# Recurrent heads that take one step per half tile of projections, with their matmuls pinned in program order on TensorE

## The chip, the cores and the metric

The kernel runs on one core of a Trainium2 chip. The metric is the time of one execution on the device in microseconds (us). The engines of a core run side by side, each with its own queue of instructions that it takes strictly in order: TensorE (PE) multiplies matrices into eight PSUM banks, VectorE (DVE) and GpSimd (POOL) do elementwise work, ScalarE (ACT) does copies, casts and functions, and SyncE (SP) issues the DMAs. An instruction that needs the result of another engine waits for it at the head of its queue, and all that is queued behind it waits too.

## The reference, cut to what matters

The model has two layers. Each layer is a feed-forward block, a mixer and a second feed-forward block, over 512 prompt tokens and 8 sample tokens (one step each for 8 sequences), which share the weights; together they are 520 columns. The mixer projects x once, runs attention, a Mamba-2 scan and an HGRN2 recurrence beside each other, projects each to the model's width, gates and adds them. The change touches the HGRN2 branch and the projections around it:

```python
h = x @ p['w_in'] + p['b_in']
q, k, v, mz, mxbc, mdt, hq, hf, hi, hg, gates = _split_cols(h)
...
oh, nhg = _hgrn2(hq, hf, hi, lb, hg_prev)       # per head: S = exp(g) * S + k^T i,  o = q S
yh = (_rmsnorm(oh, p['hg_norm_w']).reshape(b, T, HG_WIDTH) * jax.nn.silu(hg.astype(jnp.float32))).astype(x.dtype)
...
merged = g_att * (ya @ p['w_br_att']) + g_ssm * (ym @ p['w_br_ssm']) + g_hg * (yh @ p['w_br_hg'])
```

HGRN2 has 4 heads (head 0 to 3 below) of 128 x 128 state. For the prompt it starts from zero and is computed in chunks of 128 tokens; for the 8 samples it is one step from a given state each.

## The kernel before

**Tiling.** Activations lie transposed, 128 channels by 520 columns, and every product is made in two halves of 260 columns; the sample columns 512 to 519 are in half 1. `gemm` (L165) makes a half tile from three matmuls per block of 128 (L176 to L178: the high part of x by the high part of the weight, the low part of x by the high, the high by the low). `lin` (L477) takes the next weight tile, makes the half tiles and has `evac` carry each to SBUF; `lin_bias` and `lin_silu` are the two evacuations. A half tile of projections is 24 matmuls of 128 x 260.

**The heads.** `hgrn_lin` (L571) first projects ten units (the forget gates of the four heads, q, i and the gate of head 0 and 1) by halves, hands the tiles out and then is a generator over the other six units. `attention_lin` (L1049) follows with six units (k, v, four q). `hgrn_head` (L601) is a generator for one head: gate functions, products on POOL and DVE that build `hk` and `hep`; five levels of four matmuls each (`level`, L638, matmuls at L646), after each a masked copy and two multiplies on DVE (L666 is the second one of level 0, L674 that of the others); transposes of i and `hk` with their copies on ACT (L685, L686), the state products on PE (L692), the states `hst` on DVE (L693, L696), the outputs (L703 and, from `hst`, L706), squares on ACT (L711), normalising on DVE (L712 to L714), transposes (L722), and the gate (L724), after which `split` (L502) casts to a high part `yhh` on ACT (L505) and a low part on DVE (L506).

**The sample steps.** `hgrn_sample` (L728) copies the head's sample columns on DVE (L733), transposes f, k, q on PE (L737), copies them as `r8` on ACT (L739), sends them to DRAM and reads them back spread over all partitions into `smp` tiles (of which there are 6), in two halves of four sequences. Each half is one POOL multiply (L748), four DVE operations that add k by i (L751), one POOL multiply by q (L754) and four ACT sums (L757) into `s_o`. When all four steps are done `hgrn_sample_out` (L759) squares (L762), makes the mean on PE (L764), normalises on DVE (L765 to L769), and `split_samples` casts to the sample columns of the four `yhh` tiles (L513), which the first merge's half 1 reads.

**What sets the order.** `weave` (L555) runs in rounds: a round takes one step of the projections (`fill`) and then, at a higher priority, `pace` steps of every head or sample step that is alive; a head h joins at round `HG_ROUNDS[h]`, a sample step at `HG_SAMPLES[h]`. A step ends at a `yield`. Then comes `merge` (L1225) with the attention pairs woven in: for each of eight output tiles and each half a gate (24 matmuls) and the branch product over the four `yhh` / `yhl` pairs (12 matmuls). The program's order is not yet the queues' order: a tile scheduler places every instruction by its priority and its own idea of when its inputs are ready, and lets later ones pass. Only an instruction that is pinned with `keep_in_program_order` stays behind the one that the program issued before it on its engine. The PSUM banks are four of tag `g` (projections, merge), three of tag `s` (heads, attention) and one of tag `x` (sample steps).

```python
HG_ROUNDS = (0, 2, 4, 5)
HG_SAMPLES = (5, 6, 8, 10)
...
        self.weave(lins, starts, 22 - len(self.MIX_HEAD), 2)
        with self.early(3):
            self.hgrn_sample_out(l)
```

Of the kernel before, what the change touches and what calls it, by code (L numbers as in the profile page):

```python
# [43 lines left out]
HK = DT // 2  # L44
HG_ROUNDS = (0, 2, 4, 5)
AT_ROUNDS = (0, 0, 3, 3)
HG_SAMPLES = (5, 6, 8, 10)

# [77 lines left out]
class Kernel:  # L126
# [349 lines left out]

    def lin(self, evac, m=P, halves=(0, 1)):  # L477
        wt = self.w.get()
        for half in halves:
            c0, c1 = HALVES[half]  # L480
            p = self.bank()
            self.gemm(p, wt, self.xs, half, m=m)
            with self.early(1):
                evac(p[:m, : c1 - c0], c0, c1)

    def lin_bias(self, out, bias, scale=1.0, halves=(0, 1)):
        self.lin(lambda p, c0, c1: self.nc.scalar.activation(out[:, c0:c1], p, AF.Identity, bias=bias, scale=scale), halves=halves)

    def lin_silu(self, out, hbias, halves=(0, 1)):

        nc = self.nc

        def evac(p, c0, c1):
            u = self.half_tile()[:, : c1 - c0]
            t = self.half_tile()[:, : c1 - c0]
            nc.scalar.activation(u, p, AF.Identity, bias=hbias, scale=0.5)
            nc.scalar.activation(t, p, AF.Tanh, bias=hbias, scale=0.5)
            nc.vector.scalar_tensor_tensor(out[:, c0:c1], t, 1.0, u, op0=ALU.add, op1=ALU.mult)

        self.lin(evac, halves=halves)  # L500

# [25 lines left out]
    def mixer(self, l):  # L527
        self.hg_out, self.ms_out, self.at_out, self.mgs = [], [], [], []
        self.sp = {n: self.sm(32, "s_" + n) for n in ("f", "k", "q", "i", "sg", "z", "aq", "ak", "av", "y", "o")}
        self.sp["x"] = self.sm(48, "s_x")  # L530
        self.scv, self.pcv = self.sm(144, "scv"), self.sm(18, "pcv")
        self.nc.sync.dma_start(self.scv.rearrange("p (j b w) -> p j b w", b=8, w=3), self.ap["sconv"][l])
        lins = self.hgrn_lin(l)
        st = next(lins)
        aq = {}
        lins = itertools.chain(lins, self.attention_lin(l, aq))
        head = lambda h: self.hgrn_head(l, h, st)
        smp = lambda h: self.hgrn_sample(l, h, st)
        pair = lambda i: self.attention_pair(l, i, aq)

        starts = [(r, head(h)) for h, r in enumerate(HG_ROUNDS)] + [(r, smp(h)) for h, r in enumerate(HG_SAMPLES)]
        self.weave(lins, starts, 22 - len(self.MIX_HEAD), 2)
        with self.early(3):
            self.hgrn_sample_out(l)
        self.mg = self.wide("mg")
        self.weave(self.merge(l, 0, self.hg_out), [(r, pair(i)) for i, r in enumerate(AT_ROUNDS)], DT, 2)
        with self.early(3):
            self.attention_sample(l)
        self.mamba(l)
        self.weave(self.merge(l, 1, self.at_out), [], DT, 0)  # L550
# [18 lines left out]


    def hgrn_lin(self, l):  # L571
        nc = self.nc
# [4 lines left out]
        def unit(u, halves=(0, 1)):  # L577
            hb = dp[:, u : u + 1]
            if u < 4:
                self.lin_bias(T[u], pr[:, 48 + u : 49 + u], halves=halves)  # L580
                return
            h, kind = (u - 4) // 3, (u - 4) % 3
# [3 lines left out]
            if kind == 1:  # L586
                self.lin_bias(d[h], pr[:, 48 + u : 49 + u], halves=halves)
            else:
                self.lin_silu(d[h], hb, halves)

        for half in (0, 1):
            for u in self.MIX_HEAD:
                unit(u, (half,))
        yield T, q, it, sg
        for u in range(16):
            if u in self.MIX_HEAD:
                continue
            unit(u)
            yield

    def hgrn_head(self, l, h, st):  # L601
# [36 lines left out]
        def level(i):  # L638
# [5 lines left out]
            for c in range(4):  # L644
                out = p[:m, c * n : c * n + n]
                nc.tensor.matmul(  # L646
                    out.rearrange("p (b w) -> p b w", w=w) if i else out,
# [17 lines left out]
        nc.vector.tensor_tensor(ep3, ep3, tf.unsqueeze(2).to_broadcast([P, 64, 8]), op=ALU.mult)  # L665
        nc.vector.tensor_tensor(em3, em3, ts.unsqueeze(2).to_broadcast([P, 64, 8]), op=ALU.mult)  # L666
        w = 8
        for i in range(1, 5):
# [21 lines left out]
        for c in range(4):  # L690
            cs = slice(c * P, (c + 1) * P)
            nc.tensor.matmul(pst[:, cs], lhsT=ktok[:, cs], rhs=itok[:, cs], start=True, stop=True)  # L692
        nc.vector.tensor_copy(st[:, :P], pst[:, :P])  # L693
# [7 lines left out]
        for c in range(4):  # L701
            cs = slice(c * P, (c + 1) * P)
            nc.tensor.matmul(po[:, cs], lhsT=att[:, c, :], rhs=itok[:, cs], start=c == 0, stop=False)  # L703
# [16 lines left out]
        for c in range(4):  # L720
            cs = slice(c * P, (c + 1) * P)
            nc.tensor.transpose(pt[:, cs], o[:, cs], self.ident)  # L722
        yv = self.sum_slot("hy")[:, :TP]
# [4 lines left out]
    def hgrn_sample(self, l, h, st):  # L728
# [121 lines left out]
    def mamba(self, l):  # L850
# [16 lines left out]
        for j in range(4):  # L867
            self.lin_silu(z[j], dp[:, 28 + j : 29 + j])
            nc.vector.tensor_copy(self.sp["z"][:, 8 * j : 8 * j + 8], z[j][:, TP:])
# [179 lines left out]
    def attention_lin(self, l, aq):  # L1049
        nc = self.nc  # L1050
        pr = self.par[l]
        k = self.slot(name="ak")
        self.lin_bias(k, pr[:, 48 + 16 : 48 + 17])
        nc.vector.tensor_copy(self.sp["ak"][:, :8], k[:, TP:])
        nc.sync.dma_start(self.ap["o_pk"][l], k[:, TP - P : TP])
        yield
        v = self.slot(name="av")
        self.lin_bias(v, pr[:, 48 + 17 : 48 + 18])
# [3 lines left out]
        yield  # L1062
        for i in range(4):
            q = self.slot(name="aq")
            self.lin_bias(q, self.qb[l][:, i : i + 1], scale=0.125)
            nc.vector.tensor_copy(self.sp["aq"][:, 8 * i : 8 * i + 8], q[:, TP:])
            aq[i] = q
            yield

# [442 lines left out]
```

## Time and profile before

| | |
|---|---|
| median of 3 runs | 2611.08 us (2609.08 to 2611.87) |
| the profiled execution | 2615.0 us |
| its span on the core | 2613.2 us |
| PE busy | 2544.7 us (97%) |
| DVE busy | 1949.0 us (75%) |
| ACT busy | 1251.0 us (48%) |
| POOL busy | 681.6 us (26%) |

The profile is of one execution. The timeline of an engine lists start (us from the span's start), duration, engine, line, operation, tiles as out<-in, shapes and count; in square brackets stands the idle time ahead of it and what ended that. A table of waits groups the idle time of an engine by the line that waited and the line waited for. Windows give the busy time of every engine in a stretch and the granted clock of TensorE as a share of its full speed. Tile names carry no numbers in the trace. The recurrent heads of layer 0 lie at 424.5 to 560 us, those of layer 1 at 1723.6 to 1859 us.

### The profile page before, as it was taken

The numbers are of one execution on the slowest core, as the hardware profiler recorded it, in microseconds if no ns is written. First come the engines' busy times: TensorE is split into PE (matmuls) and PEld (weight loads), VectorE is DVE, ScalarE is ACT, GpSimd is POOL, SyncE is SP. The second block draws the span as 40 slices with busy tenths as digits, with TensorE's granted clock in tenths as the row PEclk, the third lists the DMA queues.
The fourth block names the chain that finished last, engine by engine and source line by source line (L and its number), as shares of the span: only waits on it lengthen the run. The fifth ranks groups of instructions, "written<-read, shape, count | busy, mean of one in ns | idle before, by whom it ended". The sixth has DMA issues, their size and how long they took to land.

```text
span 2613.2 us, 51867 instructions
## 1 busy us (share of the span) xinstructions
PE 2544.7 (97%) x20784; PEld 2477.7 (95%) x20784; DVE 1949.0 (75%) x3690; ACT 1251.0 (48%) x2358; POOL 681.6 (26%) x635
## 2 busy tenths in 40 slices
PE   8999999999999999999989999999999999999997
PEld 8999999898989999999989999999989899999997
DVE  8795888854685588868897858978546845978596
ACT  6343566443534473434663534754435344635255
POOL 2121243300143441212331212433001434312124
PEclk9999999999999999999999999999999999999999
DMA  5331446412242343232532414564123423333233
GB/s 209 111 129 66 142 162 217 149 66 82 99 138 91 122 138 107 88 114 82 186 132 86 146 57 142 175 213 138 60 86 111 138 90 123 135 100 106 89 121 123
DMA packets 134066, 318.17 MB, mean 122 GB/s; under 512 B 20452, under 2 KB 56516, under 8 KB 133824
## 3 DMA queue, kind: packets, MB, share of 16 engines
q1 hardware_dynamic: 133824, 314.86, 35.9%
q8 instruction: 163, 2.67, 0.4%
q14 instruction: 79, 0.65, 0.1%
HBM read 302.93 MB, written 11.88 MB: 120 GB/s over the span
## 4 chain that ended last, share of the span: by engine, by line
PE 72%; DVE 16%; DMA 4%; issue 3%; ACT 2%; POOL 2%; SPq 0%; POOLq 0%; ACTq 0%; DVEq 0%
PE g L176 15%; PE g L177 15%; PE g L178 15%; PE g L382 5%; PE g L384 5%; PE g L383 5%; DVE wl L91 3%; PE s L382 2%; PE s L384 2%; PE s L383 2%; DVE y L225 1%; DMA ws<-in_w_gu 1%; PE s L1098 1%; DMA smp<-r8d 1%; DVE ht L200 1%
## 5 line engine op out<-in xcount | busy, mean ns | idle before, releaser
L176 PE MATMUL g<-xh,wh 128*128 128x260 f32 (+1 forms) x2336 | 671.8, 288 | 6.6 <-ACT xh L1375 5.9
L178 PE MATMUL g<-xh,wl 128*128 128x260 f32 (+1 forms) x2336 | 669.8, 287 | 2.9 <-DVE wl L91 2.8
L177 PE MATMUL g<-xl,wh 128*128 128x260 f32 (+1 forms) x2336 | 669.5, 287 | 0.3 <-DVE xl L1376 0.3
L90 ACT CAST wh<-ws 128x1024 fp32r<-128x1024 f32 (+1 forms) x382 | 389.7, 1025 | 382.2 <-PE g L177 256.4
L91 DVE TENSOR_TENSOR wl<-ws,wh 128x1024 fp32r<-128x1024 f32 (+1 forms) x382 | 466.5, 1223 | 124.6 <-ACT wh L90 123.6
L176 PEld LDWEIGHTS g<-xh,wh 128*128 128x128 f32 (+1 forms) x2336 | 441.5, 189 | 16.4 <-issue 6.1
L178 PEld LDWEIGHTS g<-xh,wl 128*128 128x128 f32 (+1 forms) x2336 | 441.4, 189 | 10.1 <-issue 4.1
L177 PEld LDWEIGHTS g<-xl,wh 128*128 128x128 f32 (+1 forms) x2336 | 441.4, 189 | 7.9 <-issue 4.6
L73 ACT CAST wh<-ws 128x1024 fp32r<-128x1024 f32 (+1 forms) x288 | 265.4, 941 | 290.9 <-PE g L177 161.7
L178 PE MATMUL g<-hh,wl 128*128 128x260 f32 x1408 | 396.0, 283 | 0.0
L177 PE MATMUL g<-hl,wh 128*128 128x260 f32 x1408 | 395.9, 283 | 0.0
L176 PE MATMUL g<-hh,wh 128*128 128x260 f32 x1408 | 391.9, 282 | 1.9 <-DVE y L251 1.9
L74 DVE TENSOR_TENSOR wl<-ws,wh 128x1024 fp32r<-128x1024 f32 (+1 forms) x288 | 317.9, 1110 | 90.0 <-ACT wh L73 88.5
L105 POOL TENSOR_TENSOR ws<-ws 128x512 f32<-128x512 f32 x72 | 128.3, 1783 | 643.1 <-DMA ws<-in_w_gu 251.7
L176 PEld LDWEIGHTS g<-hh,wh 128*128 128x128 f32 x1408 | 262.9, 188 | 2.4 <-DVE y L251 2.3
L177 PEld LDWEIGHTS g<-hl,wh 128*128 128x128 f32 x1408 | 264.8, 188 | 0.1
L178 PEld LDWEIGHTS g<-hh,wl 128*128 128x128 f32 x1408 | 264.5, 188 | 0.2
L382 PE MATMUL g<-xh,wh 128*128 128x260 f32 x864 | 245.6, 285 | 3.3 <-ACT wh L73 3.0
L383 PE MATMUL g<-xl,wh 128*128 128x260 f32 x864 | 244.3, 284 | 0.0
L384 PE MATMUL g<-xh,wl 128*128 128x260 f32 x864 | 241.8, 283 | 0.0
L382 PEld LDWEIGHTS g<-xh,wh 128*128 128x128 f32 x864 | 163.4, 189 | 5.8 <-ACT wh L73 4.8
L382 PE MATMUL g<-sx,wh 128*128 128x260 f32 x576 | 163.3, 284 | 4.1 <-ACT wh L73 4.1
(407 smaller groups left out, 5712.2 us busy)
## 6 DMA issues: line engine op xcount, KB each, us to landing
ws<-in_w_gu SPq DMA_DIRECT2D x208, 512.0 KB
ws<-in_w_in SPq DMA_DIRECT2D x132, 512.0 KB
ws<-in_w_dn SPq DMA_DIRECT2D x96, 512.0 KB
ws<-in_w_out SPq DMA_DIRECT2D x32, 512.0 KB
ws<-in_w_dn SPq DMA_DIRECT2D x32, 384.0 KB
smp<-r8d SPq DMA_DIRECT2D x48, 256.0 KB
ws<-in_w_br SPq DMA_DIRECT2D x24, 512.0 KB
smp<-in_hgr SPq DMA_DIRECT2D x16, 256.0 KB
```

Of the source, the lines that this page charges most:

```text
L73: nc.scalar.copy(h[:, :n], s[:, :n])
L74: nc.vector.tensor_tensor(lo[:, :n], s[:, :n], h[:, :n].bitcast(F32), op=ALU.subtract)
L90: nc.scalar.copy(h[:, :n], s[:, :n])
L91: nc.vector.tensor_tensor(lo[:, :n], s[:, :n], h[:, :n].bitcast(F32), op=ALU.subtract)
L105: nc.gpsimd.tensor_tensor(pa[:, b], u[:, a], u[:, b], op=ALU.add)
L176: nc.tensor.matmul(out, lhsT=h[:, wc], rhs=xh[:, c0:c1], start=st, stop=False)
L177: nc.tensor.matmul(out, lhsT=h[:, wc], rhs=xl[:, c0:c1], start=False, stop=False)
L178: nc.tensor.matmul(out, lhsT=lo[:, wc], rhs=xh[:, c0:c1], start=False, stop=en)
L200: nc.vector.tensor_tensor(s1, self.y[0][:, c0:c1] if n == 1 else s1, y, op=ALU.add)
L382: nc.tensor.matmul(out, lhsT=h[:, wc], rhs=xh, start=first and k == 0, stop=False, **go)
L383: nc.tensor.matmul(out, lhsT=h[:, wc], rhs=xl, start=False, stop=False, **go)
L384: nc.tensor.matmul(out, lhsT=lo[:, wc], rhs=xh, start=False, stop=k == HK - 1, **go)
```

## The change

The projections become a generator that yields after each half tile (`lin_steps`), so a round is a half tile and not a tile: 24 rounds and not 12, and a head or sample step takes one step a round and not two. The rounds at which they join are rewritten. Two more `yield`s are put in: in a head after level 0's two multiplies, in a sample step after its three copies. All matmuls and transposes of the heads and the sample steps go through `mm` and `tr`, which pin them in program order. No instruction is added or removed.

```diff
-HG_ROUNDS = (0, 2, 4, 5)
+
+HG_ROUNDS = (0, 3, 7, 10)
 AT_ROUNDS = (0, 0, 3, 3)
-HG_SAMPLES = (5, 6, 8, 10)
+HG_SAMPLES = (8, 11, 14, 18)
...
-    def lin(self, evac, m=P, halves=(0, 1)):
+    def lin(self, *args, **kw):
+        for _ in self.lin_steps(*args, **kw):
+            pass
+
+    def lin_steps(self, evac, m=P, halves=(0, 1)):
         wt = self.w.get()
         for half in halves:
...
                 evac(p[:m, : c1 - c0], c0, c1)
+            yield
...
-        self.weave(lins, starts, 22 - len(self.MIX_HEAD), 2)
+        self.weave(lins, starts, 2 * (22 - len(self.MIX_HEAD)), 1)
+        for _ in lins:
+            pass
...
+    def mm(self, *args, **kw):
+        self.tc.keep_in_program_order(self.nc.tensor.matmul(*args, **kw))
+
+    def tr(self, *args):
+        self.tc.keep_in_program_order(self.nc.tensor.transpose(*args))
...
-                nc.tensor.matmul(
+                self.mm(
                     out.rearrange("p (b w) -> p b w", w=w) if i else out,
...
         nc.vector.tensor_tensor(em3, em3, ts.unsqueeze(2).to_broadcast([P, 64, 8]), op=ALU.mult)
+        yield
         w = 8
...
-                nc.tensor.transpose(p[:, cs], src[:, cs], self.ident)
+                self.tr(p[:, cs], src[:, cs], self.ident)
...
-            nc.tensor.matmul(po[:, cs], lhsT=qp[:, cs], rhs=st[:, ps], start=False, stop=c == 3)
+            self.mm(po[:, cs], lhsT=qp[:, cs], rhs=st[:, ps], start=False, stop=c == 3)
...
             nc.vector.tensor_copy(sp[n][:, sl], t[h][:, TP:])
+        yield
 
         p = self.bank("x")
         for k, n in enumerate(("f", "k", "q")):
-            nc.tensor.transpose(p[:8, k * P : (k + 1) * P], sp[n][:, sl], self.ident)
+            self.tr(p[:8, k * P : (k + 1) * P], sp[n][:, sl], self.ident)
```

What this does to the queues shows in their order. The first matmuls of level 0 of head 0 moved from row 3373 of PE's queue to row 3509; outside the heads' section and the first merge the order is the same. Line numbers of the kernel after are moved by the edit (L176 is L177, L751 is L766), and every pinned matmul carries the line of `mm` (L582), every pinned transpose that of `tr` (L585).

PE, layer 0, the transposes of the last sample step (`x`, from the small tiles `s_f`, `s_k`, `s_q`) before, among projections (`g_6419`) and level 1 of head 2 (`hep_6003`, `hk_5959`):

```order
L176 MATMUL g_6419<-xh_78,wh_6018 128x260
L646 MATMUL s_6104<-hep_6003,hk_5959 128x64 x4
L692 MATMUL s_6163<-hit_6082,hkt_6083 128x128 x4
L177 MATMUL g_6419<-xl_79,wh_6018 128x260
L178 MATMUL g_6419<-xh_78,wl_6019 128x260
L176 MATMUL g_6419<-xh_78,wh_6018 128x260
L177 MATMUL g_6419<-xl_79,wh_6018 128x260
L737 MATMUL x_6860<-ident_1015,s_f_4733 8x128
L737 MATMUL x_6860<-ident_1015,s_k_4734 8x128
L737 MATMUL x_6860<-ident_1015,s_q_4735 8x128
L178 MATMUL g_6419<-xh_78,wl_6019 128x260
```

The same transposes now (`x_6788`), with the last head's state products (`s_6720`), outputs (`s_6759`) and the first merge's product (`g_7041`):

```order
L177 MATMUL g_7041<-yhh_6662,wh_6909 128x260
L582 MATMUL s_6720<-hit_6666,hkt_6667 128x128 x4
L582 MATMUL s_6759<-hit_6666,att1_1044 128x128 x4
L178 MATMUL g_7041<-yhl_6663,wh_6909 128x260
L179 MATMUL g_7041<-yhh_6662,wl_6910 128x260
L582 MATMUL s_6759<-hst_6719,hep_6207 128x128 x3
L585 MATMUL x_6788<-ident_1015,s_f_4733 8x128
L585 MATMUL x_6788<-ident_1015,s_k_4734 8x128
L585 MATMUL x_6788<-ident_1015,s_q_4735 8x128
L585 MATMUL s_6844<-ident_1015,ho_6767 128x128 x4
L1091 MATMUL s_7097<-ident_1015,av_6402 128x128 x4
```

They moved from row 3809 of PE's queue to row 4126, behind the last head's output products.

PE, layer 0, the first branch product of half 1 (`g_7082`, which reads the sample columns of `yhh`) before, behind a whole gate (`g_7055`):

```order
L177 MATMUL g_7055<-xl_79,wh_6800 128x260
L178 MATMUL g_7055<-xh_78,wl_6801 128x260
L176 MATMUL g_7082<-yhh_5989,wh_6904 128x260
L177 MATMUL g_7082<-yhl_5990,wh_6904 128x260
L178 MATMUL g_7082<-yhh_5989,wl_6905 128x260
```

And now, with the attention's scores (L1111) and the mean of the sample output (`x_6968`) ahead of it:

```order
L1111 MATMUL s_7142<-ak_6222,aq_6538 128x256
L1111 MATMUL s_7147<-ak_6222,aq_6686 128x128
L779 MATMUL x_6968<-ssq_6966,inv_hg_1031 128x32
...
L1111 MATMUL s_7166<-ak_6222,aq_6686 128x256
L1146 MATMUL s_7301<-ident_1015,asc_7105 128x128
L177 MATMUL g_7082<-yhh_6081,wh_6909 128x260
L177 MATMUL g_7177<-xh_78,wh_7004 128x260
L178 MATMUL g_7177<-xl_79,wh_7004 128x260
```

Between the last sample transposes and this product there stood 320 rows before, and 24 now; the next gate (`g_7177`) stands behind it.

DVE, layer 0, the last head's states (`hst`) before, with the last sample multiply (L751) 68 rows ahead:

```order
L514 TENSOR_TENSOR yhl_6659<-s_o_4743,yhh_6658 128x8
L506 TENSOR_TENSOR yhl_6659<-hy_6656,yhh_6658 128x512
L693 COPY hst_6662<-s_6663 128x128
L1178 COPY qm_1040<-s_aq_4739 64x8 x2
L696 SCALAR_TENSOR_TENSOR hst_6662<-hst_6662,tw128_6521,s_6663 128x128 x3
```

And now, the multiplies of sample step 2 (`smp`) directly ahead:

```order
L766 SCALAR_TENSOR_TENSOR smp_6522<-smp_6524,s_i_4736,smp_6522 128x128 x4
L738 SCALAR_TENSOR_TENSOR hy_6660<-s_6655,par0_1046,hsg_5632 128x512
L92 TENSOR_TENSOR wl_7356<-ws_7353,wh_7355 128x1024
L514 TENSOR_TENSOR yhl_6663<-hy_6660,yhh_6662 128x512
L766 SCALAR_TENSOR_TENSOR smp_6615<-smp_6617,s_i_4736,smp_6615 128x128 x4
L707 COPY hst_6719<-s_6720 128x128
L710 SCALAR_TENSOR_TENSOR hst_6719<-hst_6719,tw128_6608,s_6720 128x128 x3
```

The states moved behind the sample multiplies that were long done before.

## Rows read from the trace of the kernel before

**Rows 1.** Page part 1: busy time, share of the span, instructions of each engine.

```profile
PE 2544.7 (97%) x20784; PEld 2477.7 (95%) x20784; DVE 1949.0 (75%) x3690; ACT 1251.0 (48%) x2358; POOL 681.6 (26%) x635
```

**Rows 2.** Windows of the heads' section in layer 0 and 1: length, then busy times.

```profile
core 0: us, PE busy (x) PEld busy (x) DVE busy (x) ACT busy (x) POOL busy (x), PEclk, DMA share, GB/s
424.50:560.00 135.50, 127.04 (x1056) 124.08 (x1054) 105.73 (x277) 63.13 (x195) 42.76 (x49) 0.99 0.48 151
...
1723.60:1859.20 135.60, 127.75 (x1063) 124.39 (x1062) 107.11 (x280) 63.91 (x196) 42.34 (x49) 0.99 0.48 154
```

**Rows 3.** Waits of PE: us in total, times, longest.

```profile
PE s L646 <- DVE hk L666: 7.7, 5, 2.5
...
PE s L646 <- DVE hk L674: 4.3, 6, 1.2
...
PE x L737 <- DVE s_q L733: 2.5, 2, 1.2
```

**Rows 4.** Timelines of five engines, layer 0: the last sample step and its reader.

```profile
496.93 0.27 PE L737 MATMUL x<-ident,s_f 128*8 128x128 f32 x1
...
499.65 0.45 ACT L739 COPY r<-x 8x384 f32<-8x384 f32 x1
...
506.82 1.33 POOL L748 TENSOR_TENSOR smp<-smp 128x512 f32<-128x512 f32 x1 [1.43 <-DMA smp<-r8d]
...
517.30 0.34 DVE L751 SCALAR_TENSOR_TENSOR smp<-smp,s_i 128x128 f32<-128x128 f32 x1
...
517.77 1.27 POOL L754 TENSOR_TENSOR smp<-smp 128x512 f32<-128x512 f32 x1 [4.16 <-DVE newton L242]
...
528.47 0.25 DVE L769 SCALAR_TENSOR_TENSOR s_o<-s_o,par,s_sg 128x32 f32<-128x32 f32 x1
...
529.22 0.38 ACT L513 CAST yhh<-s_o 128x8 fp32r<-128x8 f32 x3
...
554.08 0.28 PE L176 MATMUL g<-yhh,wh 128*128 128x260 f32 x1
```

**Rows 5.** Timeline of PE: level products, two projection matmuls, the longest wait.

```profile
424.50 1.06 PE L646 MATMUL s<-hep,hk 128*128 128x128 f32 x8
...
425.31 0.36 PE L178 MATMUL g<-xh,wl 128*128 128x260 f32 x1
...
514.74 0.28 PE L176 MATMUL g<-xh,wh 128*128 128x260 f32 x1
514.86 0.28 PE L177 MATMUL g<-xl,wh 128*128 128x260 f32 x1
...
517.52 1.61 PE L646 MATMUL s<-hep,hk 128*128 128x64 f32 x8 [2.38 <-DVE hk L666]
```

**Rows 6.** Timelines of ACT and DVE: sample step 2, the last head's states.

```profile
479.50 0.47 ACT L739 COPY r<-x 8x384 f32<-8x384 f32 x1
...
494.83 1.13 DVE L751 SCALAR_TENSOR_TENSOR smp<-smp,s_i 128x128 f32<-128x128 f32 x4
...
547.64 0.28 DVE L693 COPY hst<-s 128x128 f32<-128x128 f32 x1
...
548.21 1.12 DVE L696 SCALAR_TENSOR_TENSOR hst<-hst,tw,s 128x128 f32<-128x128 f32 x3
```

**Rows 7.** Timelines of DVE and POOL: one multiply with POOL busy and idle.

```profile
492.16 1.73 POOL L748 TENSOR_TENSOR smp<-smp 128x512 f32<-128x512 f32 x1
...
492.67 1.77 DVE L666 TENSOR_TENSOR hk<-hk,ts 128x512 f32<-128x512 f32 x1
...
516.70 0.67 DVE L666 TENSOR_TENSOR hk<-hk,ts 128x512 f32<-128x512 f32 x1
```

**Rows 8.** Timeline of DVE: an operation of the attention's scores.

```profile
568.28 0.48 DVE L1104 CUSTOM_DVE_ANT_0 asc<-s,abias,par 128x256 f32<-128x256 f32 x1
```

**Rows 9.** Window behind the longest wait; the granted clock is the third last number.

```profile
517.89:521.30 3.41, 3.41 (x18) 3.41 (x18) 3.27 (x8) 1.51 (x9) 1.15 (x1) 0.50 0.22 81
```

More of the change, by code (lines that the diff above doesn't have):

```diff
@@ L484, in lin @@
                 evac(p[:m, : c1 - c0], c0, c1)
+            yield
     def lin_bias(self, out, bias, scale=1.0, halves=(0, 1)):
-        self.lin(lambda p, c0, c1: self.nc.scalar.activation(out[:, c0:c1], p, AF.Identity, bias=bias, scale=scale), halves=halves)
+        return self.lin_steps(
+            lambda p, c0, c1: self.nc.scalar.activation(out[:, c0:c1], p, AF.Identity, bias=bias, scale=scale), halves=halves
+        )
     def lin_silu(self, out, hbias, halves=(0, 1)):
@@ L498, in evac @@
             nc.vector.scalar_tensor_tensor(out[:, c0:c1], t, 1.0, u, op0=ALU.add, op1=ALU.mult)
-        self.lin(evac, halves=halves)
+        return self.lin_steps(evac, halves=halves)
     def split(self, y, name, slot=None):
@@ L579, in unit @@
             if u < 4:
-                self.lin_bias(T[u], pr[:, 48 + u : 49 + u], halves=halves)
-                return
+                return self.lin_bias(T[u], pr[:, 48 + u : 49 + u], halves=halves)
             h, kind = (u - 4) // 3, (u - 4) % 3
@@ L586, in unit @@
             if kind == 1:
-                self.lin_bias(d[h], pr[:, 48 + u : 49 + u], halves=halves)
-            else:
-                self.lin_silu(d[h], hb, halves)
+                return self.lin_bias(d[h], pr[:, 48 + u : 49 + u], halves=halves)
+            return self.lin_silu(d[h], hb, halves)
         for half in (0, 1):
             for u in self.MIX_HEAD:
-                unit(u, (half,))
+                yield from list(unit(u, (half,)))[1:]
         yield T, q, it, sg
         for u in range(16):
[L596 to L599, printed above, removed]
+            if u not in self.MIX_HEAD:
+                yield from unit(u)
     def hgrn_head(self, l, h, st):
@@ L691, in hgrn_head @@
             cs = slice(c * P, (c + 1) * P)
-            nc.tensor.matmul(pst[:, cs], lhsT=ktok[:, cs], rhs=itok[:, cs], start=True, stop=True)
+            self.mm(pst[:, cs], lhsT=ktok[:, cs], rhs=itok[:, cs], start=True, stop=True)
         nc.vector.tensor_copy(st[:, :P], pst[:, :P])
@@ L702, in hgrn_head @@
             cs = slice(c * P, (c + 1) * P)
-            nc.tensor.matmul(po[:, cs], lhsT=att[:, c, :], rhs=itok[:, cs], start=c == 0, stop=False)
+            self.mm(po[:, cs], lhsT=att[:, c, :], rhs=itok[:, cs], start=c == 0, stop=False)
         for c in range(1, 4):
             cs, ps = slice(c * P, (c + 1) * P), slice((c - 1) * P, c * P)
-            nc.tensor.matmul(po[:, cs], lhsT=qp[:, cs], rhs=st[:, ps], start=False, stop=c == 3)
+            self.mm(po[:, cs], lhsT=qp[:, cs], rhs=st[:, ps], start=False, stop=c == 3)
         o = self.sum_slot("ho")[:, :TP]
@@ L721, in hgrn_head @@
             cs = slice(c * P, (c + 1) * P)
-            nc.tensor.transpose(pt[:, cs], o[:, cs], self.ident)
+            self.tr(pt[:, cs], o[:, cs], self.ident)
         yv = self.sum_slot("hy")[:, :TP]
@@ L867, in mamba @@
         for j in range(4):
-            self.lin_silu(z[j], dp[:, 28 + j : 29 + j])
+            for _ in self.lin_silu(z[j], dp[:, 28 + j : 29 + j]):
+                pass
             nc.vector.tensor_copy(self.sp["z"][:, 8 * j : 8 * j + 8], z[j][:, TP:])
@@ L1052, in attention_lin @@
         k = self.slot(name="ak")
-        self.lin_bias(k, pr[:, 48 + 16 : 48 + 17])
+        yield from self.lin_bias(k, pr[:, 48 + 16 : 48 + 17])
         nc.vector.tensor_copy(self.sp["ak"][:, :8], k[:, TP:])
         nc.sync.dma_start(self.ap["o_pk"][l], k[:, TP - P : TP])
-        yield
         v = self.slot(name="av")
-        self.lin_bias(v, pr[:, 48 + 17 : 48 + 18])
+        yield from self.lin_bias(v, pr[:, 48 + 17 : 48 + 18])
         nc.vector.tensor_copy(self.sp["av"][:, :8], v[:, TP:])
@@ L1061, in attention_lin @@
         aq["k"], aq["v"] = k, v
-        yield
         for i in range(4):
             q = self.slot(name="aq")
-            self.lin_bias(q, self.qb[l][:, i : i + 1], scale=0.125)
+            yield from self.lin_bias(q, self.qb[l][:, i : i + 1], scale=0.125)
             nc.vector.tensor_copy(self.sp["aq"][:, 8 * i : 8 * i + 8], q[:, TP:])
             aq[i] = q
-            yield
     def attention_pair(self, l, i, aq):
```

## The prediction

> **What bounds the kernel now.** I read the share of busy time first: TensorE (PE) is busy 97% of the span and VectorE (DVE) 75% [rows 1]. Shares over the whole span say little about one stage, so the next view is busy time by stretch. The recurrent heads run from 424.5 to 560 us in layer 0 and again from 1723.6 us in layer 1. There PE is busy 127.04 of 135.50 us and 127.75 of 135.60, so it idles 8.5 and 7.9 us, 16.3 together [rows 2]. The table of PE's waits says for what: L646, the products of the levels, on DVE's `hk` (7.7 and 4.3 us) and L737, the transposes of the sample steps, on `s_q` (2.5), 14.5 of the 16.3 us [rows 3]. So the change can win at most 16.3 us, 0.6%, by better placing, unless it speeds up PE itself, and it removes no instruction.
>
> The second thing to read is how long the work beside PE takes, since a pinned instruction makes PE wait for it. The last head's sample step of layer 0 shows it [rows 4]: transposes at 496.93, ScalarE (ACT) copies `r8` at 499.65, the DMAs bring it back broadcast, GpSimd (POOL) multiplies from 506.82, DVE ends its last L751 at 517.64, POOL multiplies again at 517.77, and DVE finishes `s_o` at 528.72. ACT casts it to the sample columns of `yhh` at 529.22. That is 29 us from `r8` to `s_o`. The first product of half 1 that reads these columns runs at 554.08, 57 us after the transposes. In the kernel before, then, all of this path is covered with 25 us to spare.
>
> **The change part by part.**
> *Nothing is added or taken away*: the same instructions run on every engine; PE's order is the same before the heads' section and again behind its first merge. Only the section's two copies move. The additional yields issue nothing by themselves.
>
> *The old waits (A).* The heads start later: level 0 of head 0 stands 136 PE instructions later, at 0.12 us each (514.74 to 514.86) [rows 5] some 16 us. Those projections only change places with others, so the shift itself costs nothing, and its cover is the 24 half tiles of projections that fill the section in both. The wait of 2.38 us at 517.52 [rows 5] and its like lie at places that no longer exist. I credit all of them: -8 us a layer.
>
> *Waits in the heads before the last projections (B).* Each sample step is now pinned on PE, and its multiplies stand on DVE's queue ahead of the next level's products. Head 2's `r8` copy at 479.50 is followed by the end of its second half of multiplies at 495.96, 16.5 us later; head 3's by 18.0 us (499.65 to 517.64) [rows 4, 6]. In the new DVE order, sample step 0's second half stands ahead of head 2's mask of level 1 and its two multiplies, which level 2 on PE waits for. Some seven operations behind it (0.67 us for a multiply [rows 7]) make 16.5 + 5 = 21.5 us. In its new order PE has between the step's transposes and that level 119 projection matmuls and 20 small ones: 119 x 0.12 + 20 x 0.2 = 18.3 us, where 0.2 is a fourth of the 0.81 us that four of them take (424.50 to 425.31) [rows 5]. Stall: some 3 us. The same pattern with sample step 1 and head 3 has 117 and 28, 19.6 us, against the same 21.5: 2 us. For the levels between them I add 2, about a quarter of the old waits. B = 7 us a layer. From below, 2: these two patterns are covered and only the last term is left. From above, 13, if most of the old waits (8 us) stay beside the 5.
>
> *The last head and the sample output (C), the main term.* In program order the last sample step comes behind head 3's output products, and head 3's states `hst` stand on DVE behind the second half of sample step 2. From sample step 2's transposes, which now stand behind head 2's last products, PE can only reach the first half-1 product through this chain:
> (a) sample step 2 to its last multiply, 16.5 us as above, then `hst` at 547.64 and 548.21, 0.28 + 1.12 = 1.4 us [rows 6]; with some of it begun early, 17 [14 to 18];
> (b) head 3's output products, transposes of the last sample step and the copy `r8`: 1.5;
> (c) `r8` to `s_o`: 29 us in the trace, less what DVE's and POOL's waits for head work cost there. The row at 517.77 shows 4.16 us of POOL waiting for DVE's queue [rows 4]. I take 26 [19 to 32];
> (d) the cast and its start, 0.2.
> Sum 44.7 us. What PE has in the new order between these two points: 53 projection matmuls (6.4 us) and 55 small ones (11.0 us), 17.4 us. The merge cannot fill the rest: the next gate's matmuls (`g_7177`) stand behind that product in PE's queue. C = 44.7 - 17.4 = 27 us a layer [19 to 35].
> In the kernel before the same path had 57 us of cover. ACT's table load and the exponentials of the attention, which stand ahead of the cast in ACT's new order, run while the path waits and are not added.
>
> *What is behind (D).* The attention pairs come later: one of their custom operations on DVE takes 0.48 us [rows 8], and eight of them stand ahead of the division. A little of it is late for PE's transposes: +1 [0 to 2]. Nothing else is fed by the merge's end but the next projections, whose weights are prefetched by then.
>
> *The clock (E).* After the wait of 2.38 us that ends at 517.52 the granted clock is 0.50 of full speed (1.2 GHz) in the 3.41 us to 521.3, with PE busy all the time [rows 5, 9]. Such a stretch loses half of it, 1.7 us. A stall of 27 us in place of several short ones gives one or two such stretches more: +2 [0 to 3].
>
> Sum by layer: -8 + 7 + 27 + 1 + 2 = +29 us; with both layers +58. The profiled execution took 2615.0 us (span 2613.2) and the median is 2611.08, 3.9 us less. 2615.0 + 58 - 3.9 = **2669 us**. All low ends: -8 + 2 + 19 + 0 + 0 = 13, twice 26, 2637. All high ends: -8 + 13 + 35 + 2 + 3 = 45, twice 90, 2701.
>
> **The rivals.**
> *R1, the pins cover every wait.* If program order puts enough projections between a step and the next, PE never waits in the heads: 2611.08 - 16.3 = 2595 us. For it: the heads' own waits are short, none over 2.5 us [rows 3], and the steps are now spread over 24 rounds. Against it: the path from the last sample step's transposes to the first half-1 product would have to fit into the PE work that stands between them, 3 projection matmuls and 25 small ones, 5.4 us, and the trace has 29 us for it [rows 4]. It decides below that. Chance 0.05.
>
> *R2, the sample paths run at their own pace.* Once the heads are done, DVE and POOL have nothing else. The path's own operations are then a POOL multiply of 1.3 us for each half, two L751 of 1.1 us, POOL again 1.3, and DMA legs as in [rows 4]: `r8` to the first POOL multiply is 7.2 us. C falls to its lower end of 19 and B to 4: -8 + 4 + 19 + 1 + 1 = 17 a layer, 2615.0 + 34 - 3.9 = 2645 us. For it: part of the 29 us are waits, as POOL's 4.16. Against it: the second half starts its DMAs only when the buffers of the step before are free. Chance 0.17.
>
> *R3, POOL's products slow DVE more than before.* The same multiply L666 takes 1.77 us at 492.67, beside POOL's multiply at 492.16 (1.73 us), and 0.67 us at 516.70 with POOL idle [rows 7]. Sample steps pinned among the levels put more of POOL's products beside DVE's: seven such meetings in a layer, 1.1 us each, on a path that PE now waits for, are +8 a layer. By it the time is 2669 + 16 = 2685 us. Against it: POOL's products are the same in number, and they ran beside DVE before too. Chance 0.13.
> The Trainium skill (SBUF — State Buffer, "Who interferes with whom") states that DVE and GpSimd share a pair of ports as an exclusive lock, and that an operation of DVE with two inputs in SBUF contends with GpSimd's reads; the two rows of L666 agree with it. By that rule alone, R3 would come about wherever the two meet.
>
> *R4, the new waits only equal the old.* 2611 us: B and C together 8 us a layer. This is what comes out if the sample path is not what PE waits for, since another order of the merge's banks lets the gates of half 0 run on. In the new order they stand behind. Chance 0.05.
>
> **How the numbers follow.** Forecast 0.60, R2 0.17, R3 0.13, R1 0.05, R4 0.05. The measurement tells some 0.2% (5 us) from no change. Faster by more than that is R1: 0.05. Within it is most of R4: 0.04. Slower: 0.60 + 0.17 + 0.13 + 0.01 = 0.91. The forecast's own range is 2637 to 2701; the range given reaches a little lower, to 2630, to take in R2 with the bounds of its terms, and leaves out R1, R4 and the upper end of R3.
>
> **What would show it.** In the trace after: PE's waits in the heads' section some 35 us a layer instead of 8, the longest ahead of the first half-1 product of `yhh` (on ACT's cast, or on attention transposes in its place), near 20 us or more; a second one on `hst` for head 3's output products (a); level waits on `hk` in head 2 and 3 of 2 to 4 us (B); a granted clock of half behind them. The stretch from the last sample transposes to the first half-1 product, 57 us before, would be some 30. If the table of waits has no wait over 5 us in the heads, C is wrong, and R1 or R4 holds; if C is there but near 15, R2.

## The result and the profile after

The changed kernel takes 2644.47 us (median of 4 runs, 2639.9 to 2645.91) against 2611.02 for the kernel before: a ratio of 1.0124, 95% interval [1.0111, 1.0137]. It is slower by 33 us. The forecast was 2669 us with a range of 2630 to 2701: the side and the range hold, the size was nearly twice too large.

Page part 1 of the changed kernel, busy time, share and instructions of each engine; it answers to [rows 1]:

```profile
span 2644.1 us, 51871 instructions
PE 2553.9 (97%) x20784; PEld 2489.2 (94%) x20784; DVE 1939.8 (73%) x3690; ACT 1249.8 (47%) x2358; POOL 681.5 (26%) x635
```

The span grew by 30.9 us (2613.2 to 2644.1). PE's busy time grew by 9.2 us with the same 20784 instructions, so its idle time grew by 21.7. The share of PE, 97%, is what it was before: a share over the span does not show the loss.

The waits of PE in the whole execution, in us, times and the longest; the lines of other stages, which differ little between the two kernels, are left out. It answers to [rows 3]:

```profile
PE s L585 <- DVE ho L728: 15.4, 2, 8.1
...
PE s L1111 <- DVE am L1117: 8.7, 2, 5.2
PE g L177 <- ACT yhh L513: 7.2, 2, 4.5
...
PE s L582 <- DVE hst L707: 2.5, 3, 1.0
PE x L779 <- ACT ssq L777: 2.3, 2, 1.5
...
PE g L178 <- DVE yhl L514: 2.0, 3, 0.9
...
PE s L1146 <- DVE asc L1136: 1.4, 2, 0.7
...
PE s L582 <- DVE hk L688: 0.2, 1, 0.2
```

The old waits of the levels on `hk` (12 us) and of the sample transposes on `s_q` (2.5) are gone but for 0.2 us: what the pins were to do for the levels, they did. New ones stand at the end of the heads: the transposes of the last heads' outputs on `ho`, the attention's scores (L1111), the first products on `yhh`, the mean of the sample output (L779). No line is for the half-1 product on the sample output's cast: waits that stand ahead of it in PE's queue have taken its time.

Windows of the heads' section of layer 0 (length, busy time by engine, granted clock third from the end):

```profile
424.50:533.00 108.50, 107.51 (x913) 106.16 (x912) 85.10 (x207) 52.39 (x136) 28.82 (x41) 1.00 0.42 134
533.00:552.00 19.00, 14.39 (x115) 12.80 (x113) 13.48 (x37) 7.06 (x26) 4.76 (x3) 0.99 0.57 158
552.00:559.00 7.00, 0.00 (x0) 0.00 (x0) 2.47 (x13) 2.63 (x17) 1.26 (x1) 0.50 0.33 123
559.00:581.00 22.00, 14.37 (x46) 9.38 (x46) 13.39 (x60) 9.14 (x38) 5.02 (x4) 0.50 0.47 132
581.00:585.50 4.50, 4.33 (x20) 4.33 (x21) 3.25 (x18) 1.70 (x10) 0.00 (x0) 0.50 0.00 0
585.50:600.00 14.50, 14.50 (x142) 14.04 (x141) 8.20 (x19) 7.67 (x21) 0.00 (x0) 0.99 0.11 34
```

Up to 533 us, PE idles 1.0 us of 108.5; in the section of [rows 2] it idled 8.5. From there to 581 us it idles 19.2 us of 48, and from 552 to 585.5 us the granted clock is half (1.2 GHz).

What holds PE up there is read on ACT's timeline and, last line, POOL's (start, duration, in brackets the idle time before and what ended it):

```profile
546.74 0.30 ACT L772 ACTIVATE smp<-smp 128x128 f32<-128x128 f32 x1
...
553.79 0.31 ACT L772 ACTIVATE smp<-smp 128x128 f32<-128x128 f32 x1 [6.66 <-POOL smp L769]
...
554.97 0.25 ACT L725 ACTIVATE ho<-s 128x128 f32<-128x128 f32 x1
...
555.97 0.45 ACT L754 COPY r<-x 8x384 f32<-8x384 f32 x1
...
580.95 0.49 ACT L521 CAST yhh<-s_o 128x8 fp32r<-128x8 f32 x4 [1.03 <-DVE s_o L784]
...
552.50 1.26 POOL L769 TENSOR_TENSOR smp<-smp 128x512 f32<-128x512 f32 x1 [4.73 <-DMA smp<-r8d]
```

ACT's queue has the sums of sample step 2 (L772) ahead of the squares of head 3's output (L725) and of the copy `r8` of the last sample step (L754). The sums wait 6.66 us for POOL, and POOL waited 4.73 us for a broadcast read. So head 3's normalised output is late, PE waits 8.1 us for it at its transposes, and the last sample step starts late too. The path that the forecast followed is there from end to end: sample step 2's transposes at 533.08, `hst` finished at 550.71, `r8` copied at 555.97, the cast at 580.95, and the first half-1 product at 581.30:

```profile
533.08 0.27 PE L585 MATMUL x<-ident,s_f 128*8 128x128 f32 x1
...
550.71 0.27 PE L585 MATMUL x<-ident,s_f 128*8 128x128 f32 x1
...
559.33 0.87 PE L585 MATMUL s<-ident,ho 128*128 128x128 f32 x3 [8.13 <-DVE ho L728]
...
570.49 3.45 PE L1111 MATMUL s<-ak,aq 64*128 64x256 f32 x12 [5.18 <-DVE am L1117]
...
581.30 0.57 PE L177 MATMUL g<-yhh,wh 128*128 128x260 f32 x1
```

From the last sample transposes to that product it is now 30.6 us (550.71 to 581.30), where [rows 4] has 57. DVE's timeline has the ends of two links, and between them the last sample step's multiplies (L766), which hold DVE's operations on the attention's scores (L1117) until 570.09; PE waits 5.2 us for these. The idle time ahead of L766 is put down to another read, but the POOL product that it takes in ends at 568.01 (566.75 + 1.26), just before its start:

```profile
549.60 1.11 DVE L710 SCALAR_TENSOR_TENSOR hst<-hst,tw,s 128x128 f32<-128x128 f32 x3
...
568.05 2.12 DVE L766 SCALAR_TENSOR_TENSOR smp<-smp,s_i 128x128 f32<-128x128 f32 x4 [3.59 <-DMA abias<-in_c_abias]
...
580.67 0.25 DVE L784 SCALAR_TENSOR_TENSOR s_o<-s_o,par,s_sg 128x32 f32<-128x32 f32 x1
```

### The profile page after: what moved, and what is told of

Its sections match the earlier page's. It is cut to its first block, busy times and chain, and to the rows that moved or that the text cites. A ratio compares the mean times of both kernels' runs of the same rounds, so it can differ in the third digit from the quotient of the medians.

```text
span 2644.1 us, 51871 instructions
## 1 busy us (share of the span) xinstructions
PE 2553.9 (97%) x20784; PEld 2489.2 (94%) x20784; DVE 1939.8 (73%) x3690; ACT 1249.8 (47%) x2358; POOL 681.5 (26%) x635
## 4 chain that ended last, share of the span: by engine, by line
PE 77%; DVE 12%; DMA 4%; ACT 2%; issue 2%; POOL 2%; SPq 0%; POOLq 0%; ACTq 0%; DVEq 0%
PE g L177 16%; PE g L178 16%; PE g L179 16%; PE g L383 6%; PE g L385 6%; PE g L384 6%; DVE wl L92 3%; PE s L383 2%; PE s L385 2%; PE s L384 2%; DMA smp<-r8d 2%; PE s L582 1%; DVE y L226 1%; DVE ht L201 1%; DVE xl L230 1%
## 5 line engine op out<-in xcount | busy, mean ns | idle before, releaser
L177 PE MATMUL g<-xh,wh 128*128 128x260 f32 (+1 forms) x2336 | 671.9, 288 | 6.9 <-ACT xh L1388 5.7
L177 PEld LDWEIGHTS g<-xh,wh 128*128 128x128 f32 (+1 forms) x2336 | 443.1, 190 | 13.9 <-ACT xh L1388 5.7
L177 PE MATMUL g<-hh,wh 128*128 128x260 f32 x1408 | 392.1, 283 | 1.6 <-DVE y L252 1.6
L106 POOL TENSOR_TENSOR ws<-ws 128x512 f32<-128x512 f32 x72 | 134.7, 1871 | 645.0 <-DMA ws<-in_w_gu 255.1
L177 PEld LDWEIGHTS g<-hh,wh 128*128 128x128 f32 x1408 | 263.3, 188 | 2.2 <-DVE y L252 2.1
```

The lines of the kernel that those rows point to most:

```text
L106: nc.gpsimd.tensor_tensor(pa[:, b], u[:, a], u[:, b], op=ALU.add)
L177: nc.tensor.matmul(out, lhsT=h[:, wc], rhs=xh[:, c0:c1], start=st, stop=False)
```

## The experiments

The theory to test: the loss comes from the sample steps, pinned late in the program, whose chain PE has to wait out; the heads' pins by themselves are cheap. Rivals: the half-tile rounds and their pace cost the time; or the heads' own chain at the end does. All ratios are against the kernel before, run on the same chip in the same batch (2613.47, 2615.03 and 2613.77 us).

**Pins alone.** The kernel before, its rounds as they were, with `mm` and `tr`:

```diff
-                nc.tensor.matmul(
+                self.mm(
...
-                nc.tensor.transpose(p[:, cs], src[:, cs], self.ident)
+                self.tr(p[:, cs], src[:, cs], self.ident)
```

> The kernel before with its own rounds and pace, and only the pins added (all matmuls and transposes of heads and sample steps in program order). Theory P (the pins of the sample steps make the last sample step late, and the half-1 product waits for it): in PE's new order 6 projection matmuls and 44 small ones stand between the last sample transposes and the first half-1 product, where the kernel before has 292 and 89, so PE waits there as in the changed kernel: 2635 to 2655 us, with PE waits of some 20 us a layer at the end of the heads. Rival T (the half-tile rounds and the pace cost the time, the pins do not): within 5 us of 2611.

Measured: 2671.7 us, ratio 1.0226 [1.0203, 1.025]. Slower even than expected, and 27 us slower than the whole change. PE idles 110.0 us of the profiled span of 2670.0, 41.5 more than before, so theory P's wait of some 20 us a layer is met in size; its busy time grew by 15.3 us as well. With the pins in place, the rounds of the change take back part of the harm.

**Rounds alone.** The changed kernel with the pins out:

```diff
-        self.tc.keep_in_program_order(self.nc.tensor.matmul(*args, **kw))
+        self.nc.tensor.matmul(*args, **kw)
...
-        self.tc.keep_in_program_order(self.nc.tensor.transpose(*args))
+        self.nc.tensor.transpose(*args)
```

> The changed kernel with the pins taken out; half-tile rounds, pace 1, start rounds and the two yields stay. Theory P: 298 projection matmuls and 79 small ones stand between the last sample transposes and the first half-1 product, so there is no long wait: 2605 to 2616 us, the old short waits of some 8 us a layer are back. Rival T: 2635 us or more.

Measured: 2624.62 us, ratio 1.0038 [1.0025, 1.0052]. A miss for both: not the same as before, and far from 2635. The rounds cost some 10 us on their own. PE's busy time is 2551.5 us against 2544.7 before, 6.8 us more with the same instructions. The waits of PE on the sample output show one place:

```profile
PE x L779 <- ACT ssq L777: 5.8, 2, 2.9
```

The mean of the sample output now makes PE wait 2.9 us a layer, and the clock falls behind it (window of that place, columns as above):

```profile
526.00:530.00 4.00, 3.70 (x20) 3.70 (x20) 3.89 (x13) 1.47 (x4) 0.00 (x0) 0.62 0.37 131
```

**Heads pinned, sample steps free.**

```diff
-            self.tr(p[:8, k * P : (k + 1) * P], sp[n][:, sl], self.ident)
+            nc.tensor.transpose(p[:8, k * P : (k + 1) * P], sp[n][:, sl], self.ident)
```

> The changed kernel with the sample steps' transposes alone not pinned; the heads stay pinned. 203 projection matmuls and 66 small ones stand between the last sample transposes and the first half-1 product, about 38 us at 0.12 and 0.2 us each. Theory P: the long wait is gone and most of the 8 us a layer of old waits stays away: 2597 to 2607 us, faster than before. Rival H (the pins of the heads cost as much: ACT's squares of the last head and its output transposes are late in any case): 2620 to 2632 us, with a PE wait of some 8 us on the last head's output in each layer.

Measured: 2633.62 us (2624.52 to 2634.38, the profiled execution 2624.52), ratio 1.0065 [1.0043, 1.0088]. The theory's 2597 to 2607 is a miss; the time is a little above rival H's 2620 to 2632, and its wait is smaller. Unpinning the sample steps takes back about half of the loss (1.0124 to 1.0065), but the wait on the last head's output stays, 4.4 us in each layer in place of 8.1 and 7.3, and level waits come back. Against the rounds alone (1.0038) the heads' pins cost some 7 us more, but the two intervals overlap. The waits:

```profile
PE s L585 <- DVE ho L728: 11.6, 4, 4.4
...
PE s L582 <- DVE hk L688: 7.4, 3, 3.7
...
PE x L779 <- ACT ssq L777: 4.4, 2, 3.2
```

**All pinned, sample steps earlier.**

```diff
-HG_SAMPLES = (8, 11, 14, 18)
+HG_SAMPLES = (3, 6, 10, 13)
```

> The changed kernel with all pins, the sample steps put earlier in the program: they join at rounds 3, 6, 10, 13 in place of 8, 11, 14, 18. In PE's order 22 projection matmuls and 46 small ones stand between the last sample transposes and the first half-1 product in place of 3 and 29, some 6 us more cover. Theory P: the loss shrinks by about that and by what the earlier multiplies no longer hold up on DVE and ACT: 2618 to 2632 us. Rival (the place of the sample steps does not matter, only the chain of the last head does): within 4 us of 2644.

Measured: 2640.83 us, ratio 1.0109 [1.0078, 1.0139]. A miss: within 4 us of the changed kernel, as the rival said. But the reason is not that the place does not matter. The waits on the scores and on L779 are gone from the table of waits; the one on `ho` has grown to 9.9 us in layer 0 and 11.5 in layer 1. DVE's timeline says why; it is head 2's norm (L726 to L244, 4 columns wide, and its use in L728) with the last sample step's multiplies (L766) in the middle of it:

```profile
548.31 1.14 DVE L766 SCALAR_TENSOR_TENSOR smp<-smp,s_i 128x128 f32<-128x128 f32 x4 [1.15 <-POOL smp L763]
...
550.04 0.16 DVE L726 TENSOR_SCALAR hss<-hss 128x4 f32<-128x4 f32 x1
550.23 0.17 DVE L239 TENSOR_SCALAR hr<-hss 128x4 int32<-128x4 int32 x1
553.02 1.28 DVE L766 SCALAR_TENSOR_TENSOR smp<-smp,s_i 128x128 f32<-128x128 f32 x4 [2.62 <-DMA smp<-r8d]
554.23 0.16 DVE L240 TENSOR_SCALAR hr<-hr 128x4 int32<-128x4 int32 x1
...
556.20 0.69 DVE L728 TENSOR_TENSOR ho<-s,hr 128x512 f32<-128x512 f32 x1
```

ACT had finished the squares, from which the norm starts, at 547.69. One half of the sample step's multiplies (548.31) stands ahead of the norm and waits for POOL, the other (553.02) stands within it and waits for a read; PE waits behind all of it. Theory and rival share the blame: it is the sample steps' work, but by way of the queues of DVE and ACT, not only by the length of its own path.

**The sample output cut.** The sample output's norm and gate are left out and the sample columns filled with the projected gate.

```diff
-        o, sq = sp["o"], self.sm(32, "ssq")
...
-        self.split_samples(o, self.hg_out)
+        self.split_samples(sp["sg"], self.hg_out)
```

> The changed kernel without the sample output's square, mean, norm and gate: the sample columns of the branch's input are taken from the projected gate instead, which is ready early; the sample steps themselves stay. Left out: that part of the samples' HGRN2 output. Theory C (the half-1 product waits for the sample output): PE's waits on the attention's scores, the mean and the product (10 us a layer in the first layer with their slow clock behind) go, the wait of 7 to 8 us on the last head's normalised output stays: 2618 to 2632 us. Rival Q (all of the loss is the sample steps' work standing ahead of the heads' on DVE and ACT): within 5 us of 2644.

Measured: 2626.62 us (2618.16 to 2631.17, the profiled execution 2618.16), ratio 1.0039 [1.0025, 1.0053], in the range of theory C. The sample output is worth some 18 to 22 us of the 33. Not all of that is the wait for the last link: the wait on `ho` fell as well, from 15.4 to 5.7 us in the two layers together, which was not expected. With the output gone, the order of the last steps is another one.

**The samples' work cut.** In addition, the broadcast reads and all work of the sample steps on POOL, DVE and ACT behind the copy `r8` are left out:

```diff
-            nc.gpsimd.tensor_tensor(s3, s3, fb, op=ALU.mult)
...
-                nc.scalar.activation(kb[:, b], qb[:, b], AF.Copy, accum_out=sp["o"][:, c : c + 1])
```

> As the run with the output cut, and the sample steps' broadcast reads, POOL, DVE and ACT work left out as well (transposes, copy and the state's load and store stay; the state is not updated). Theory Q in part: with that work gone from the queues of DVE and ACT the wait on the last head's output falls from 8 us to 3 to 5 us (squares, scale and multiply of that head alone): 2603 to 2616 us. Rival H (the heads' own chain at the end, pinned back to back, makes that wait): the wait stays at 7 us or more and the time at 2618 us or more.

Measured: 2600.85 us, ratio 0.9942 [0.9924, 0.996], a little below theory Q's range. The wait on `ho` is 1.5 us in the two layers together; the heads' own chain, pinned back to back, does not make it by itself:

```profile
PE s L585 <- DVE ho L728: 1.5, 2, 0.7
```

**The same cut in the kernel before**, as the control:

> The kernel before with the same work of the sample steps and of their output left out as in the cut of the changed kernel (which took 2601 us). If the changed order is as good as the old one once the samples' work is out of the queues of DVE and ACT, this takes 2600 to 2606 us too: only the light work is saved, and the 33 us that the change costs are all owed to the sample steps. If the changed order is better by its 16 us of old head waits, this stays at 2608 to 2613 us. If it is worse even without samples: 2595 us or less.

Measured: 2592.79 us, ratio 0.9919 [0.9907, 0.9931], the last of the three expected cases. So the samples' work, with the order that it brings, costs the kernel before 0.8%, 21 us, and the changed kernel 1.8% (1.0124 to 0.9942), 44 us by the medians and some 47 by the ratios. Of the 33 us of the change, some 25 are thus owed to the samples' work. Without it the changed order is still 6 to 8 us slower (ratios 0.9942 and 0.9919, medians 2600.85 and 2592.79), from two batches whose intervals overlap. The window of the heads' section in the control, layer 0 and 1:

```profile
424.50:600.00 175.50, 175.50 (x1436) 165.82 (x1436) 113.48 (x319) 76.57 (x185) 18.32 (x33) 1.00 0.23 75
1723.00:1900.00 177.00, 177.00 (x1408) 163.59 (x1407) 108.18 (x325) 73.22 (x187) 11.74 (x22) 1.00 0.21 68
```

PE does not idle at all. The 16 us of old waits, most of which look like waits of the heads on their own levels in [rows 3], are gone with the samples' work. In the cut of the changed kernel the same windows have PE idle for 2.0 us each at a clock of 0.98.

**Heads earlier.** Two kernels with heads at rounds 0, 2, 5, 8 and sample steps at 3, 5, 8, 12: one with only the heads pinned, one with all. At these rounds head 2 writes the mask tile that it shares with head 0 before head 0 has read it, so the prompt's part of the output changes; the instructions are the same.

```diff
-HG_ROUNDS = (0, 3, 7, 10)
+HG_ROUNDS = (0, 2, 5, 8)
...
-HG_SAMPLES = (8, 11, 14, 18)
+HG_SAMPLES = (3, 5, 8, 12)
```

> The kernel with only the heads pinned, heads joining at rounds 0, 2, 5, 8 in place of 0, 3, 7, 10, sample steps not pinned. 338 projection matmuls and 86 small ones stand between the last sample transposes and the first half-1 product (203 and 66 with the later rounds). Theory (the loss grows with how late the last head and the last sample step come): 2605 to 2620 us, less than the 2624 to 2634 of the later rounds. Rival (the pins cost by themselves, by waits on the levels): 2625 us or more.

> The changed kernel, everything pinned, heads joining at rounds 0, 2, 5, 8 and sample steps at 3, 5, 8, 12. 48 projection matmuls and 47 small ones stand between the last sample transposes and the first half-1 product (3 and 29 in the changed kernel). Theory: some 9 us more cover a layer, 2622 to 2638 us. Rival (earlier heads only run into DVE, which is busy three quarters of the stretch, and the waits move to the levels): 2640 us or more.

Measured: 2629.13 us, ratio 1.0049 [1.0032, 1.0065], and 2651.49 us, ratio 1.0135 [1.0117, 1.0154]. Both rivals hold. More projections behind the last sample step do not help when the heads run into each other: with all pinned, the table of waits has L582 on `att` at 13.0 us (longest 5.5) and L779 at 7.4.

**The multiplies on POOL.** Since DVE's queue is held up by multiplies that wait for a read, they were put on POOL, in the changed kernel, in the kernel before and in the one with only the heads pinned; all work is kept.

```diff
-            for b in range(4):
-                c = 8 * h + b0 + b
-                nc.vector.scalar_tensor_tensor(s3[:, b], kb[:, b], sp["i"][:, c : c + 1], s3[:, b], op0=ALU.mult, op1=ALU.add)
+            i4 = sp["i"][:, 8 * h + b0 : 8 * h + b0 + 4].unsqueeze(2).to_broadcast([P, 4, P])
+            nc.gpsimd.tensor_tensor(kb, kb, i4, op=ALU.mult)
+            nc.gpsimd.tensor_tensor(s3, s3, kb, op=ALU.add)
```

> The changed kernel, all work kept; the sample steps' four multiply-adds on DVE are made by two operations on POOL instead (some 1.3 us each), so that no operation on DVE waits for the broadcast reads. Theory D (DVE's queue, blocked by these multiplies, holds up the heads' states and norms): the chain from the third sample step to the last head's states shrinks by 5 to 10 us a layer, 2622 to 2636 us. Rival S (ACT's sums and the final output hold PE up just as long, and POOL's longer queue adds to it): 2640 us or more.

> The kernel before with the sample steps' multiply-adds on POOL in the same way. Theory D: the old waits on the levels, which stand behind these multiplies on DVE, fall from 12 us in both layers to some 5: 2600 to 2609 us, better than both kernels. Rival R (POOL's products beside DVE slow DVE's two-input operations, or head products wait behind sample products on POOL): 2612 us or more.

> The kernel with only the heads pinned (2624 to 2634 us) with the sample steps' multiply-adds on POOL. Theory D: the waits on the last heads' norms (12 us in both layers) and levels (7 us) fall by half: 2610 to 2622 us. Rival R: 2625 us or more.

Measured: 2665.83 us, ratio 1.0201 [1.0188, 1.0214]; 2640.55 us, ratio 1.0106 [1.0092, 1.0121]; 2641.02 us, ratio 1.0104 [1.0088, 1.0119]. Theory D falls in all three as a remedy: each got slower than the kernel that it was made from, by 21, 27 and 7 us (the last with intervals that touch at 1.0088). In the kernel before with this edit, DVE beside POOL reads (DVE's timeline, then POOL's of the same time):

```profile
512.63 0.16 DVE L712 TENSOR_SCALAR hss<-hss 128x4 f32<-128x4 f32 x1
512.82 1.14 DVE L238 TENSOR_SCALAR hr<-hss 128x4 int32<-128x4 int32 x1
513.99 0.96 DVE L239 TENSOR_SCALAR hr<-hr 128x4 int32<-128x4 int32 x1
514.99 1.20 DVE L241 TENSOR_TENSOR newton<-hr 128x4 f32<-128x4 f32 x1
516.22 1.19 DVE L242 SCALAR_TENSOR_TENSOR newton<-newton,hss 128x4 f32<-128x4 f32 x1
...
520.89 0.15 DVE L242 SCALAR_TENSOR_TENSOR newton<-newton,hss 128x4 f32<-128x4 f32 x1
```

```profile
512.63 1.30 POOL L748 TENSOR_TENSOR smp<-smp 128x512 f32<-128x512 f32 x1
513.89 1.04 POOL L750 TENSOR_TENSOR smp<-smp,s_i 128x512 f32<-128x512 f32 x1
514.89 1.28 POOL L754 TENSOR_TENSOR smp<-smp 128x512 f32<-128x512 f32 x1
516.12 1.26 POOL L751 TENSOR_TENSOR smp<-smp 128x512 f32<-128x512 f32 x1
```

The same operation L242 takes 1.19 us beside POOL's product and 0.15 with POOL idle. Four operations of 4 columns take 4.5 us here; each ends within 0.03 us of the end of the POOL product beside which it runs (L238 at 513.96, the product at 513.93). PE's next level waits 5.3 us behind them.

## Why the prediction was right, and where its size was not

*The bound and the old waits (A).* Right: -16.3 us was credited, and 0.2 of the waits on `hk` is left. Their cause was misread, though without harm to the sum: in the control they go with the samples' work.

*Waits in the heads (B).* Mis-sized: 7 us a layer was forecast, and up to the last projections PE waits 1.0 us, for `hst`, in layer 0. The pattern is there, sample step 0's second half ahead of head 2's multiplies on DVE. The step that failed is the chain's length: 21.5 us was put down, and from the transposes at 483.50 to the end of L688 for level 2 (500.29 + 0.42) it took 17.2, because the multiplies ended 12.9 us after `r8` (484.02 to 495.81 + 1.14) and not 16.5. The 2 us for the levels in between did not come either. The cover held: the level ran at 501.36, 17.9 us after the transposes, against 18.3 forecast.

*The last chain (C).* The mechanism and its links are as forecast, and its length nearly so: 44.7 us was the sum, and from 533.30 to 581.30 it is 48.0. Link by link: (a) 17 forecast, 17.4 measured to the end of `hst`; (b) 1.5 forecast, 5.3 measured to the start of `r8`, because of ACT's sums ahead of it, which the forecast did not look for on that queue; (c) 26 forecast, 25.0 measured (555.97 to 580.92); (d) 0.2 and 0.4. What failed is the cover: 17.4 us of PE work was counted, and PE was busy for 29 of the 48 us. It ran 14.4 of them (559 to 581) at half clock, which accounts for some 7 of the 11 us; and the small matmuls took longer than 0.2 us (four from 546.01 to 547.00, 0.25 each). So the waits of C were 18.6 and 17.7 us in the two layers and not 27. They lie below its stated bounds of 19 to 35, but these do not follow from the links: their low ends give 14 + 1.5 + 19 + 0.2 - 17.4 = 17.3, their high ends 34.3. The sign that was named, one wait near 20 us ahead of the half-1 product or of attention transposes, did not come. The wait is in several pieces, and the longest, 8.1 and 7.3 us, is on `ho` at head 3's transposes, behind the same late sums of ACT that lengthened link (b).

*Behind (D)* was right: 0.7 us a layer on L1146. *The clock (E)* was too small: 2 us a layer was forecast. In layer 0 PE does 18.7 us of work at half clock (14.37 + 4.33, from 559 to 585.5), which at full clock would take about half (the starts of successive projection matmuls are 0.22 us apart at 581.66 and 0.12 at 588.05). So some 9 us, an estimate from these, go to the clock, most of them inside the chain. The clock is at half from 552 to 585.5 us, not for one or two short stretches. C and E are in part one sum seen twice: work at half clock within the chain fills what would otherwise be a wait. The busy time of the whole execution grew by only 9.2 us; what took the rest back is not shown.

Over both layers by the trace: A -16.3, waits on `hst` and `hk` in the heads +2.0, C +36.3, D +1.4, and for E the growth of busy time, +9.2, together +32.6 against 30.9 in the spans and 33 in the medians. Forecast were -16, +14, +54, +2 and +4: B and C were too large by 12 and 18 us, and E too small by 5.

*The rivals.* R1 and R4 are out. R2 named 2645 us, and C = 19 a layer is what came; but its reason, that the path runs at its own pace once the heads are done, is not what happened: the path took as long as forecast, and that its number came so near is luck. R3 is not what the changed kernel shows (DVE's busy time fell from 1949.0 to 1939.8 us), but its mechanism is real and shows in the kernel before with the multiplies on POOL; how much of the loss of the three runs with POOL it makes was not tried apart. The Trainium skill (SBUF — State Buffer, "Who interferes with whom") states that the order of issue, not the shape of an operation, decides which of DVE and GpSimd blocks; the rows of that run agree, where operations of 4 columns wait for products of 512.

What stays open: the 6 to 8 us by which the changed order is slower without the samples. The two profiled executions are 13.4 us apart, 8.6 of it PE's busy time (2542.4 and 2533.8 us) and the rest its idle time; that it is the clock was not tried apart. A version that keeps all work and beats both kernels was not found.

## What to carry to other kernels

Before a step is pinned in an engine's queue, follow what it starts on the other engines to the next thing that the pinned engine waits for, and count the independent work that is left in between: here 57 us between the last sample transposes and their reader became 31, half of it waiting. A wait named after one tile may be owed to another chain that sits ahead of it in a queue; cutting that chain out of both kernels is the run that shows it. And small work that waits for a DMA should not stand in a queue ahead of a chain that the busiest engine needs, nor be moved to POOL beside a DVE that is busy three quarters of the time.

## What the runs showed of the hardware that was not expected

Operations of DVE of 128 x 4 elements, which take 0.15 to 0.17 us, took 0.96 to 1.20 us each beside POOL products of 1.04 to 1.30 us, in the kernel before with the multiplies on POOL. The loss is not in proportion to their size: they lose 0.8 to 1.0 us each, and the multiply of 128 x 512 in [rows 7] loses 1.1.

The granted clock stayed at 0.50 from 552 to 585.5 us in layer 0, though PE was busy 14.4 of the 22 us from 559 to 581 and 4.33 of the 4.5 us behind it. It was idle from 552 to 559. Behind the 2.38 us wait of [rows 5] half clock lasted 3.4 us [rows 9].
